# A hybrid encoder layer on one core: normalised tokens split in token rows and turned by transposing DMA transfers

## The chip, the core and the metric

The kernel runs on one core of one Trainium2 chip. A core has a matrix engine (TensorE, "PE" in the profile, with its weight loads as "PEld"), three elementwise engines (VectorE "DVE", ScalarE "ACT", GpSimd "POOL"), a queue engine (SyncE, "SP") that issues most transfers, and 16 DMA engines that carry them out. TensorE reads its operands from the on-chip memory SBUF and writes to PSUM. The metric is the device time of one execution in microseconds; lower is better.

## The reference

One layer over 2048 tokens of width 1024. Everything reads the same normalised tokens `h` through one input projection, and that is all that the change touches.

```python
def rms_norm(x, w):
    y = x32 * lax.rsqrt(jnp.mean(x32 * x32, axis=-1, keepdims=True) + EPS)
    return (y * w)

h = rms_norm(x, norm_pre_w)                       # (2048, 1024)
proj = h @ w_in                                   # (2048, 5648)
aq, ak, av, bqkv, ba, bb, mq, z = jnp.split(proj, pts, axis=-1)
# A: grouped-query attention on aq, ak, av; B: gated DeltaNet on bqkv, ba, bb
# M: cross-attention of mq into the memory tokens, whose keys and values are
mkv = rms_norm(mem, mem_norm_w) @ w_mem_kv        # (256, 1024)
x = x + rms_norm((concat([y_a, y_b, y_m]) * silu(z)) @ w_out, norm_post_w)
```

## The kernel before

Products of float32 precision are made from float16 parts: a number is split into a rounded part "hi" and a remainder "lo", and a product is the sum of three float16 products (hi·hi, hi·lo, lo·hi). The normalised tokens are needed with the 1024 channels on the partitions; that tensor, `hT`, is four tiles of 512 tokens (`hT0` to `hT3`), each with a hi and a lo part for eight blocks of 128 channels. `hT` is the operand of every projection: `tok_proj` takes 128 tokens of it as the stationary operand, `chan_proj` and `b_proj` take 512 tokens of it as the moving one.

The first stage (pool `s0`, about the first 118 us) does three things side by side.

- The memory tokens: `mem_load(g)` fetches a quarter of `w_mem_kv` in two halves (`mraw`, two buffers), ACT rounds each (`whi`), DVE or POOL makes the remainder (`wlo`), and `mem_group(g)` multiplies (tiles `mem`, 48 products in each of four groups).
- The tokens, in 16 blocks of 128. `tok_norm` loads two blocks (`x`, four buffers), ACT sums their squares (`jk_x`), DVE takes the inverse root in some eleven small operations (`rs_x`, `rs_u`, `rst`) and scales (`h`, three buffers). `tok_turn` turns a block with eight TensorE transposes into PSUM (`tp`); from there ACT writes the hi part and DVE the lo part into `hT`.
- The values: `av_proj` multiplies a turned block with 272 columns of weights (`av`, 24 products), ACT takes it out of PSUM (`ab`, `vt`), DVE takes a maximum (`vmax`), and SP stores `vt` to `v`.

A loop over blocks writes them in this order, with the turning two blocks and the values four blocks behind the loading:

```python
if i < TB and i % 2 == 0:
    tok_norm(i)
if 0 <= i - 2 < TB:
    tok_turn(i - 2)
if 0 <= i - 4 < TB:
    av_proj(i - 4)
```

The order on each engine is not this one: a scheduler that works on a model of the times reorders the instructions of every engine when the kernel is built, and each engine then runs its own list strictly in order, waiting for semaphores. SP is such a list too: a transfer that waits holds back all that stand behind it.

Two short chains cross the engines in this stage: the scale of the memory keys (`p2mk`) and that of the memory values (`p2mv`) each need a DVE maximum, a TensorE transpose, a DVE maximum, a TensorE product and four small DVE operations.

After this stage come the query and key projections with rotation (`q`, `qt`), the convolution and DeltaNet branch (`b` and others), the gates (`z`), and attention. Attention already uses transposing transfers: `low` sends the split probabilities `hl` (128 x 4096 float16, 32 blocks of 128 x 128; `hla` in the profile) through one `dma_start_transpose` on SP into `PT`.

Of the kernel before, what the change touches and what calls it, by code (L numbers as in the profile page):

```python
# [14 lines left out]
F16 = mybir.dt.float16  # L15
I32 = mybir.dt.int32
AF = mybir.ActivationFunctionType
ALU = mybir.AluOpType
# [5 lines left out]
D = 1024  # L24
# [4 lines left out]
KC = D // 128  # L29
# [8 lines left out]
def hybrid_layer(ctx: ExitStack, tc: tile.TileContext, t: dict, out, dbg=None):  # L38
    nc = tc.nc
# [17 lines left out]
    V, G, A, T, Q = (Engine(e) for e in (nc.vector, nc.gpsimd, nc.scalar, nc.tensor, nc.sync))  # L57
# [132 lines left out]
    hpool = ctx.enter_context(tc.tile_pool(name="hT", bufs=1))  # L190
# [12 lines left out]
    hT = []  # L203
# [35 lines left out]
    def chan_proj(ps, wg, u, tb4):  # L239
        n = 0  # L240
        for kc in range(KC):
            hi, lo = (w[:, kc % 4, u * 128:u * 128 + 128] for w in wg[kc // 4])
            for wt, ht in ((hi, 0), (hi, 1), (lo, 0)):
                T.matmul(ps, wt, hT[tb4][ht][:, kc, :], start=(n == 0), stop=(n == 3 * KC - 1))
                n += 1
                if n < 3 * KC:
                    yield
# [11 lines left out]
        return load_w(src, sum(n for _, n in segs), fac, fetch)  # L259

    def tok_proj(ps, wg, tb):
        hh, hl = hT[tb // 4]
        sl = slice((tb % 4) * 128, (tb % 4) * 128 + 128)
        n = 0
        for kc in range(KC):
            hi, lo = wg[kc // 4]
            for ht, wt in ((hh, hi), (hh, lo), (hl, hi)):
                T.matmul(ps, ht[:, kc, sl], wt[:, kc % 4, :], start=(n == 0), stop=(n == 3 * KC - 1))
                n += 1


    with tc.tile_pool(name="s0", bufs=1) as p:
# [5 lines left out]
        def turned(h, dst_hi, dst_lo, name):  # L278
            for half in range(2):
                ps = tp_ps(f"tp_{name}_{half}", (128, 4, 128))  # L280
                for k in range(4):
                    T.transpose(ps[:, k, :], h[:, (half * 4 + k) * 128:(half * 4 + k + 1) * 128], ident)
                split_evac(ps, dst_hi[:, half * 4:half * 4 + 4], dst_lo[:, half * 4:half * 4 + 4])
# [36 lines left out]
        for j in range(2):  # L320
            sl = slice(j * 128, j * 128 + 128)
# [31 lines left out]
        for g in range(4):  # L353
# [2 lines left out]
                wav, (avcs,) = load_group([(1280, 256), (3072, 16)], dma)  # L356
            mem_group(g, wg)
            wg = nxt
        hT.extend(hpool.tile([128, 2, KC, 512], F16, tag="B16", name=f"hT{b}", bufs=6, align_bytes=512).rearrange("p i k c -> i p k c") for b in range(4))
        hs = {}  # L360

        def tok_norm(tb):
# [10 lines left out]
                hs[tb + j] = scaled(xs[j], wpre, rst[:, j:j + 1], f"{tb + j}")  # L373

        def tok_turn(tb):
            sl = slice((tb % 4) * 128, (tb % 4) * 128 + 128)
            turned(hs.pop(tb), hT[tb // 4][0][:, :, sl], hT[tb // 4][1][:, :, sl], f"{tb}")

        def av_proj(tb):
            ps = mm_ps(f"av{tb}")  # L380
# [130 lines left out]
    with tc.tile_pool(name="s2", bufs=1) as p:  # L511
        wg, bcs, xbs, svs, kts_ = {0: nxt[0]}, {0: nxt[1]}, {}, {}, {}

        def b_proj(ch, b):
            g, u = ch // 2, ch % 2
            if u == 1 and b == 0:
                if g < 5:
                    wg[g + 1], bcs[g + 1] = load_group([(1536 + 256 * (g + 1), 256)])
                else:
                    wg[6] = z_load(4)  # L520
            if b == 0:
                xb = xbs[ch] = p.tile([128, S + 4], F32, tag="xb", name=f"xb{ch}", bufs=2)
                V.memset(xb[:, 0:2], 0.0)
                V.memset(xb[:, S + 2:S + 4], 0.0)
            ps = mm_ps(f"b{ch}_{b}")
            n = 0
            for kc in range(KC):
                hi, lo = wg[g][kc // 4]
                sl = slice(u * 128, u * 128 + 128)
                for wt, ht in ((hi, 0), (hi, 1), (lo, 0)):  # L530
                    T.matmul(ps, wt[:, kc % 4, sl], hT[b][ht][:, kc, :], start=(n == 0), stop=(n == 3 * KC - 1))
                    n += 1
            A.activation(xbs[ch][:, 2 + 512 * b:2 + 512 * (b + 1)], ps, AF.Copy, scale=bcs[g][0])

# [262 lines left out]
    with tc.tile_pool(name="s3a", bufs=1) as sv0:  # L797
        p = rows
# [685 lines left out]
```

## Time and profile before

| | |
|---|---|
| median of 3 runs | 2539.05 us (2533.95 to 2544.41) |
| the profiled execution: time / span of its trace | 2539.24 us / 2537.5 us |
| TensorE busy, share of the span | 2368.3 us, 93% |
| VectorE busy | 1827.2 us, 72% |
| ScalarE busy | 1270.5 us, 50% |
| GpSimd busy | 626.1 us, 25% |
| first `av` product / first `q` product after the stage | 52.32 us / 117.84 us |

A busy share is an average over stages with different limits. All times below are microseconds from the start of the span; a row "start, length" gives when a piece of work began and how long it ran, and a "[1.65 <-ACT whi]" behind it means that the engine had been idle for 1.65 us before and what ended that. Rows that merge several instructions show their count as "x12". Ends of TensorE rows overlap the next one, so a rate is best read from one start to the next.

### The profile page before, as it was taken

How to read it: one execution, taken by the hardware profiler on the slowest of the kernel's cores; microseconds unless marked ns; L12 is line 12 of the kernel's file. 1: busy time of each engine (PE TensorE's matmuls, PEld its weight loads, DVE VectorE, ACT ScalarE, POOL GpSimd, SP SyncE). 2: the span in 40 equal slices, each digit the busy share in tenths (PEclk: the TensorE clock that was granted, in tenths of full speed). 3: DMA queues.
4: the chain of work that ended last, by engine and by line, in shares of the span. 5: the costliest groups of instructions: out<-in, count | busy, mean ns of one | idle time of the engine just before them, and what ended most of it. 6: DMA issues, size and time to landing. Idle time of an engine off the chain costs nothing.

```text
span 2537.5 us, 42839 instructions
## 1 busy us (share of the span) xinstructions
PE 2368.3 (93%) x15989; PEld 1619.0 (64%) x15997; DVE 1827.2 (72%) x3434; ACT 1270.5 (50%) x2496; POOL 626.1 (25%) x450
## 2 busy tenths in 40 slices
PE   6989999999999898998999898899989899999998
PEld 6778974555444356666654566566656566778887
DVE  7778768999658835545545899999999899453332
ACT  5533335544443134554645776777778778211110
POOL 2154431112111220111121333333345333111110
PEclk9999999999999999999999999999999999999999
DMA  6431213234488456767766999999999999864441
GB/s 226 144 92 63 84 59 86 83 111 125 135 257 221 135 153 203 217 200 242 239 200 183 214 222 226 203 225 215 219 227 227 227 221 209 249 223 153 150 161 42
DMA packets 867375, 448.50 MB, mean 177 GB/s; under 512 B 639072, under 2 KB 816736, under 8 KB 866912
## 3 DMA queue, kind: packets, MB, share of 16 engines
q1 hardware_dynamic: 854720, 402.78, 61.4%
q0 software_dynamic: 12448, 43.00, 5.0%
q8 instruction: 126, 2.06, 0.3%
q14 instruction: 81, 0.66, 0.1%
HBM read 195.01 MB, written 108.07 MB: 119 GB/s over the span
## 4 chain that ended last, share of the span: by engine, by line
PE 27%; DVE 15%; issue 5%; DMA 4%; ACT 2%; SPq 1%; POOL 1%; ACTq 0%; DVEq 0%; POOLq 0%
PE o L51 12%; DVE mxa L51 7%; PE sa L51 6%; DVE hla L51 4%; PE pva L51 3%; PE z L51 3%; DVE misc L51 1%; DMA PT<-hla 1%; ACT Pa L51 1%; DMA Od<-oo 1%; DMA n<-NI 1%; DMA xx<-bx 1%; DVE mxm L51 1%; DMA wor<-in_w_out 1%; SPq L51 1%
## 5 line engine op out<-in xcount | busy, mean ns | idle before, releaser
L51 PEld LDWEIGHTS <-wparts 128*128 128x128 f16 x3072 | 293.9, 98 | 326.4 <-issue 15.8
L51 PE MATMUL sa<-K,qa 128*128 128x512 f16 x1536 | 375.2, 380 | 39.1 <-ACT Pa L51 36.4
L51 ACT ACTIVATE Pa<-sa,mxa,undo 128x1024 f32<-128x1024 f32 x256 | 305.9, 1199 | 189.2 <-DVE mxa L51 146.9
L51 PE MATMUL pva<-PT,V 128*128 128x256 f16 x3072 | 382.0, 275 | 13.0 <-DMA PT<-hla 12.1
L51 PE MATMUL z<-hT,wparts 128*128 128x512 f16 x1536 | 372.4, 383 | 0.3
L51 PEld LDWEIGHTS <-V 128*128 128x128 f16 x3072 | 301.3, 99 | 104.8 <-issue 21.9
L51 DVE TENSOR_REDUCE mxa<-sa 128x1 f32<-128x1024 f32 x256 | 305.4, 1212 | 42.8 <-PE sa L51 42.5
L51 PE MATMUL o<-wo,mhl 128*128 128x512 f32 x1416 | 328.4, 393 | 6.9 <-DVE mhl L51 2.6
L51 POOL TENSOR_TENSOR hla<-Pa,hla 128x768 f16<-128x768 f32 x128 | 215.2, 1681 | 452.8 <-ACT hla L51 367.9
L51 PEld LDWEIGHTS o<-wo,mhl 128*128 128x128 f32 x1416 | 266.1, 189 | 68.5 <-DVE mhl L51 3.9
L51 DVE TENSOR_TENSOR hla<-Pa,hla 128x1280 f16<-128x1280 f32 x128 | 279.4, 2183 | 6.8 <-ACT hla L51 5.1
L51 PEld LDWEIGHTS <-qa 128*128 128x128 f16 x1536 | 150.3, 98 | 178.1 <-issue 49.2
L51 PE MATMUL b<-hT,wparts 128*128 128x512 f16 x1152 | 256.8, 379 | 0.0
L51 ACT CAST hla<-Pa 128x2048 f16<-128x2048 f32 x128 | 242.3, 1893 | 9.4 <-DMA PT<-hla 9.4
L51 PEld LDWEIGHTS <-hT 128*128 128x128 f16 x2304 | 226.0, 98 | 31.6 <-DVE hT L51 1.2
L51 PE MATMUL q<-wparts,hT 128*128 128x256 f16 x1920 | 215.8, 275 | 0.0
L51 POOL TENSOR_SCALAR wraw<-wraw,wsc 128x1024 f32<-128x1024 f32 (+1 forms) x22 | 67.5, 3066 | 348.5 <-DVE wy L51 271.0
L51 DVE SCALAR_TENSOR_TENSOR y<-xb,convw,y 128x512 f32<-128x512 f32 x192 | 145.4, 772 | 1.7
L51 ACT CAST mhl<-mr 128x2048 fp32r<-128x2048 f32 (+1 forms) x16 | 29.2, 1826 | 228.6 <-PE o L51 210.3
L51 DVE TENSOR_TENSOR mhl<-mr,mhl 128x2048 fp32r<-128x2048 f32 (+1 forms) x16 | 35.1, 2191 | 134.8 <-ACT mhl L51 134.8
L77 POOL DMA_DIRECT2D gate<-zg x64 | 35.5, 554 | 374.6 <-DVE zg L51 205.5
L51 POOL TENSOR_TENSOR mg<-mg 128x1024 f32<-128x1024 f32 (+1 forms) x16 | 35.1, 2196 | 259.0 <-DMA mg<-r 222.9
(328 smaller groups left out, 3330.6 us busy)
## 6 DMA issues: line engine op xcount, KB each, us to landing
xx<-bx SPq DMA_DIRECT2D x64, 512.0 KB, 5.1
wraw<-in_w_in POOLq DMA_DIRECT2D x42, 512.0 KB, 5.5
gate<-zg POOLq DMA_DIRECT2D x64, 256.0 KB, 4.0
NI<-nit SPq DMA_DIRECT2D x32, 512.0 KB, 4.0
mr<-mix SPq DMA_DIRECT2D x13, 1024.0 KB, 5.6
x<-in_x SPq DMA_DIRECT2D x16, 512.0 KB, 4.9
qT<-qo SPq DMA_DIRECT2D x32, 256.0 KB, 2.5
qa<-qT SPq DMA_DIRECT2D x32, 256.0 KB, 3.5
```

The costliest lines, as they stand in the source:

```text
L51: ins = f(*args, **kw)
L77: nc.gpsimd.dma_start(to, of)
```

## The change

`tok_turn` no longer uses TensorE. A block `h` is split while it still has tokens on the partitions: ACT writes the hi part and DVE the lo part of a float16 tile `h16` (128 x 2 x 1024, two buffers), both from SBUF to SBUF. One transposing transfer on SP then turns its 16 blocks of 128 x 128 into `hT`. To receive it, `hT` is laid out as [partition, block of tokens, part, channel block, 128 tokens], so that one block of tokens is contiguous; a product that reads 512 tokens now reads four pieces of 128 that lie 4 KB apart. Nothing is left out of the computation.

```diff
-                T.matmul(ps, wt, hT[tb4][ht][:, kc, :], start=(n == 0), stop=(n == 3 * KC - 1))
+                T.matmul(ps.rearrange("p (b c) -> p b c", c=128), wt, hT[tb4][:, :, ht, kc, :], start=(n == 0), stop=(n == 3 * KC - 1))
...
-        hh, hl = hT[tb // 4]
-        sl = slice((tb % 4) * 128, (tb % 4) * 128 + 128)
+        hh, hl = (hT[tb // 4][:, tb % 4, i] for i in range(2))
...
-                T.matmul(ps, ht[:, kc, sl], wt[:, kc % 4, :], start=(n == 0), stop=(n == 3 * KC - 1))
+                T.matmul(ps, ht[:, kc, :], wt[:, kc % 4, :], start=(n == 0), stop=(n == 3 * KC - 1))
...
-        hT.extend(hpool.tile([128, 2, KC, 512], F16, tag="B16", name=f"hT{b}", bufs=6, align_bytes=512).rearrange("p i k c -> i p k c") for b in range(4))
+        hT.extend(hpool.tile([128, 4, 2, KC, 128], F16, tag="B16", name=f"hT{b}", bufs=6, align_bytes=512) for b in range(4))
...
         def tok_turn(tb):
-            sl = slice((tb % 4) * 128, (tb % 4) * 128 + 128)
-            turned(hs.pop(tb), hT[tb // 4][0][:, :, sl], hT[tb // 4][1][:, :, sl], f"{tb}")
+
+            h = hs.pop(tb)
+            h16 = p.tile([128, 2, D], F16, tag="h16", name=f"h16_{tb}", bufs=2, align_bytes=512)
+            A.copy(h16[:, 0], h)
+            V.tensor_tensor(h16[:, 1], h, h16[:, 0], op=ALU.subtract)
+            nc.sync.dma_start_transpose(hT[tb // 4][:, tb % 4].rearrange("p i k c -> p (i k) c"), h16.rearrange("p i c -> p (i c)"))
```

`b_proj` changes as `chan_proj` does. Beyond the first stage every engine's list is the same row for row; within it the scheduler has moved rows. In the names below, `x10`, `h16_6`, `vt4`, `av6` are those of token block 10, 6, 4 and 6.

The SP list, from the store of the fourth block of values to the last turned block. Before:

```order
L51 DMA v_65<-vt3_823 128x256
L51 DMA x11_948<-in_x 128x1024
L51 DMA x12_1087<-in_x 128x1024
L51 DMA v_65<-vt4_894 128x256
L51 DMA x13_1091<-in_x 128x1024
L51 DMA v_65<-vt5_938 128x256
L51 DMA v_65<-vt6_1009 128x256
L51 DMA x14_1202<-in_x 128x1024
L51 DMA x15_1206<-in_x 128x1024
L51 DMA v_65<-vt7_1053 128x256
```

Now, at the same place, the stretch that carries blocks 6 and 7 and the loads of 12 and 13:

```order
L51 DMA mv16_69<-mv16_668 128x2048
L380 DMA_TRANSPOSE hT1_480<-h16_6_794 128x16x128
L380 DMA_TRANSPOSE hT1_480<-h16_7_828 128x16x128
L51 DMA v_65<-vt5_858 128x256
L51 DMA x12_987<-in_x 128x1024
L51 DMA x13_991<-in_x 128x1024
L380 DMA_TRANSPOSE hT2_481<-h16_8_889 128x16x128
L51 DMA v_65<-vt6_919 128x256
L380 DMA_TRANSPOSE hT2_481<-h16_9_923 128x16x128
L51 DMA v_65<-vt7_953 128x256
```

and, directly behind it, the stretch with the last two loads:

```order
L380 DMA_TRANSPOSE hT2_481<-h16_10_1012 128x16x128
L51 DMA v_65<-vt8_1042 128x256
L51 DMA x14_1082<-in_x 128x1024
L380 DMA_TRANSPOSE hT2_481<-h16_11_1046 128x16x128
L51 DMA v_65<-vt9_1076 128x256
L51 DMA x15_1086<-in_x 128x1024
L380 DMA_TRANSPOSE hT3_482<-h16_12_1107 128x16x128
L51 DMA v_65<-vt10_1137 128x256
L380 DMA_TRANSPOSE hT3_482<-h16_13_1141 128x16x128
L51 DMA v_65<-vt11_1171 128x256
L51 DMA v_65<-vt12_1205 128x256
L380 DMA_TRANSPOSE hT3_482<-h16_14_1175 128x16x128
```

The loads of the last two blocks stood behind the store of the seventh block of values (`vt6`); now they stand behind the stores of the ninth and tenth (`vt8`, `vt9`) and behind the turning of block 11.

The DVE list from the scale of the memory values to the blocks behind it, now:

```order
L51 COPY p2mmv_656<-p2mv_659 128x1
L51 TENSOR_SCALAR p2emv_657<-p2mmv_656 128x1
L51 TENSOR_SCALAR scales_99<-p2emv_657 128x1
L51 TENSOR_SCALAR undo_100<-p2emv_657 128x1
L51 SCALAR_TENSOR_TENSOR h_6_695<-x6_674,rst6_673,wpre_117 128x1024
L51 SCALAR_TENSOR_TENSOR h_7_697<-x7_678,rst6_673,wpre_117 128x1024
L51 SCALAR_TENSOR_TENSOR mv16_668<-mvt_207,scales_99,mv16_668 128x1024
L51 TENSOR_REDUCE vmax_96<-vt4_824 128x1
L51 TENSOR_TENSOR h16_6_794<-h_6_695,h16_6_794 128x1024
```

Block 6 is scaled right behind that chain, as it was before; but the chain's product on TensorE (`p2mv` from `ones`), which stood in the third block of values, now stands in the fifth, behind eight of `av4`'s 24 products.

## Rows read from the trace of the kernel before

**Rows 1.** The page's first part: busy time, share of the span and instructions of an engine.

```profile
PE 2368.3 (93%) x15989; PEld 1619.0 (64%) x15997; DVE 1827.2 (72%) x3434; ACT 1270.5 (50%) x2496; POOL 626.1 (25%) x450
```

**Rows 2.** Busy time of each engine in four stretches of the first stage; the columns are PE, PEld, DVE, ACT, POOL (with instructions), then TensorE's granted clock (1 is 2.4 GHz, 0.5 is 1.2), the busy share of the DMA engines and GB/s.

```profile
38.00:47.00 9.00, 7.32 (x34) 7.06 (x35) 8.69 (x23) 6.06 (x10) 4.27 (x2) 0.50 0.49 166
47.00:58.00 11.00, 11.00 (x91) 10.60 (x91) 6.50 (x13) 2.32 (x4) 4.10 (x3) 0.98 0.53 179
58.00:88.00 30.00, 30.00 (x261) 25.91 (x259) 22.98 (x58) 20.43 (x46) 0.00 (x0) 1.00 0.44 144
88.00:118.00 30.00, 25.70 (x218) 21.29 (x218) 22.91 (x55) 17.13 (x38) 7.99 (x6) 1.00 0.43 139
```

**Rows 3.** TensorE in order of time through the stage: start, length, work.

```profile
35.63 0.50 PE L51 MATMUL mem<-whi,mT 128*128 128x256 f32 x2 [1.65 <-ACT whi L51]
37.89 0.58 PE L51 MATMUL mem<-wlo,mT 128*128 128x256 f32 x1 [1.75 <-DVE wlo L51]
38.27 0.63 PE L51 MATMUL mem<-whi,mT 128*128 128x256 f32 x2
...
38.91 0.63 PE L51 MATMUL mem<-whi,mT 128*128 128x256 f32 x2
...
42.66 2.77 PE L51 MATMUL tp<-ident,h 128*128 128x128 f32 x12
45.08 0.56 PE L51 MATMUL mem<-wlo,mT 128*128 128x256 f32 x1
...
53.26 0.40 PE L51 MATMUL mem<-whi,mT 128*128 128x256 f32 x2
...
53.61 0.40 PE L51 MATMUL mem<-whi,mT 128*128 128x256 f32 x2
...
57.21 2.14 PE L51 MATMUL av<-wparts,hT 128*128 128x272 f16 x17
59.19 0.60 PE L51 MATMUL tp<-ident,h 128*128 128x128 f32 x4
59.63 2.94 PE L51 MATMUL av<-wparts,hT 128*128 128x272 f16 x24
...
77.78 0.60 PE L51 MATMUL tp<-ident,h 128*128 128x128 f32 x4
...
109.62 8.39 PE L51 MATMUL av<-wparts,hT 128*128 128x272 f16 x71
117.84 3.77 PE L51 MATMUL q<-wparts,hT 128*128 128x256 f16 x33
```

**Rows 4.** Groups of instructions between 20 and 120 us: count, busy time, mean ns of one, idle time before them.

```profile
L51 PE MATMUL av<-wparts,hT 128*128 128x272 f16 x384 | 48.3, 279 | 1.5 <-DVE hT L51 0.9 <-ACT hT L51 0.6
...
L51 DVE TENSOR_TENSOR hT<-tp,hT 128x512 f16<-128x512 f32 x32 | 20.9, 681 | 0.5 <-ACT hT L51 0.5
L51 DVE SCALAR_TENSOR_TENSOR h<-x,rst,wpre 128x1024 f32<-128x1024 f32 x16 | 20.1, 1280 | 0.6 <-DMA mkT<-mk 0.5
L51 PE MATMUL tp<-ident,h 128*128 128x128 f32 x128 | 18.7, 288 | 2.5 <-DVE wy L51 1.1 <-DVE h L51 0.8 <-DVE hT L51 0.6
L51 ACT CAST hT<-tp 128x512 f16<-128x512 f32 x32 | 17.4, 588 | 1.2 <-PE tp L51 1.2
...
L51 ACT ACTIVATE jk_x<-x 128x1024 bf16<-128x1024 f32 x13 | 13.7, 1057 | 14.0 <-DMA x<-in_x 14.0
...
L51 DVE TENSOR_REDUCE vmax<-vt 128x1 f32<-128x256 f32 x16 | 6.6, 413 | 8.1 <-ACT vt L51 8.0
...
L51 DVE TENSOR_TENSOR wlo<-mraw,whi 128x1024 fp32r<-128x1024 f32 x3 | 3.7, 1217 | 0.0
```

**Rows 5.** The transposing transfers of attention (`PT`): SP's time for one (min/median/max ns), the time to landing; the DVE remainders beside POOL in attention; and the token loads of 512 KB each between 20 and 120 us, their median time to landing.

```profile
L1158 SPq DMA_TRANSPOSE PT<-hla x128: 3844/4294/8226, 1376.0 to 2169.0; - x128
...
DMA to landing us min/median/max: 5.5/6.4/11.1
...
L51 DVE TENSOR_TENSOR hla<-Pa,hla x128: 1477/2230/2866, 1373.6 to 2164.0; 128x1280 f16<-128x1280 f32 x128
...
x<-in_x SPq DMA_DIRECT2D x12, 512.0 KB, 3.8
```

**Rows 6.** TensorE on moving operands of two pieces (`pva`, from `PT`) and of one piece (`q`), each up to the start of the next row.

```profile
1622.86 1.47 PE L51 MATMUL pva<-PT,V 128*128 128x256 f16 x12
1624.17 1.46 PE L51 MATMUL sa<-K,qa 128*128 128x512 f16 x6
...
299.75 8.68 PE L51 MATMUL q<-wparts,hT 128*128 128x256 f16 x78
308.26 1.04 PE L51 MATMUL qt<-ident,qr 128*128 128x128 f32 x8
```

**Rows 7.** Other engines in order of time: the last remainder of the memory weights on POOL; an ACT cast of 128 x 1024 from SBUF; small DVE operations of the inverse root; SP's issue of the last two token loads.

```profile
47.08 2.43 POOL L51 TENSOR_TENSOR wlo<-mraw,whi 128x1024 fp32r<-128x1024 f32 x1 [4.81 <-ACT whi L51]
...
101.75 1.06 ACT L51 CAST wparts<-wraw 128x1024 f16<-128x1024 f32 x1
...
83.69 0.16 DVE L51 TENSOR_TENSOR rs_u<-rs_u,rs_x 128x2 f32<-128x2 f32 x1
83.89 0.16 DVE L51 SCALAR_TENSOR_TENSOR rst<-rs_u,rst 128x2 f32<-128x2 f32 x1
...
86.72 1.53 SPq L51 DMA_DIRECT2D x<-in_x  x2
```

More of the change, by code (lines that the diff above doesn't have):

```diff
@@ L530, in b_proj @@
                 for wt, ht in ((hi, 0), (hi, 1), (lo, 0)):
-                    T.matmul(ps, wt[:, kc % 4, sl], hT[b][ht][:, kc, :], start=(n == 0), stop=(n == 3 * KC - 1))
+                    T.matmul(ps.rearrange("p (b c) -> p b c", c=128), wt[:, kc % 4, sl], hT[b][:, :, ht, kc, :], start=(n == 0), stop=(n == 3 * KC - 1))
                     n += 1
```

## The prediction

> **What bounds the kernel now.** I read the busy shares first: TensorE is busy for 93% of the span [rows 1], so time that it gets back counts unless something else takes its place. The change touches the first 118 us alone, so I then read the stretches of that stage [rows 2]. From 58 to 88 us TensorE has work for all 30.00 us while VectorE is at 22.98 and the DMA engines are below half. From 88 to 118 it has 25.70 of 30. In this stretch TensorE ends last, and nearly the only engine that waits for transfers is ScalarE, 14.0 us for token loads [rows 4]. Before 47 us it is the other way round: TensorE waits for ACT and DVE to split the memory weights (1.65 and 1.75 us) and runs at half clock [rows 2, 3].
>
> The stage ends for TensorE at 117.84, when the first `q` product starts [rows 3]. Everything behind stands in the same order as before, and its loads wait for the end of this stage, so I take it that a shift of this end moves the whole rest by the same amount. The question is where that end will lie.
>
> **What the change removes.** TensorE loses 128 transposes. Four of them take 0.44 us from 59.19 to 59.63, 0.11 each; twelve at half clock take 2.42 us from 42.66 to 45.08 [rows 3]. That is 116 × 0.11 + 2.42 = 15.2 us. On ACT two casts of 0.59 from PSUM go and one of 1.06 from SBUF comes; on DVE two remainders of 0.68 go and one of 128 x 1024 comes, for which the nearest row is `wlo` with 1.22 [rows 4, 7]. If POOL is active beside it, the row for attention bounds it: 2.23 for 1280 columns, 1.8 for 1024 [rows 5]. I take 1.22, since POOL has nothing to do from 58 to 88 us [rows 2]. ACT and DVE thus keep their load.
>
> **What it adds.** Sixteen transposing transfers on SP. None of this size is in the trace. The nearest are those of attention with twice the blocks: SP is held 4.29 us (median), the data has landed after 6.4 [rows 5]. By halves: SP 2.15, then a tail of 6.4 − 4.3 = 2.1, so 4.2 from issue to landing. Bounds: 3.2, if everything halves, and 6.4, if nothing does; those rows come from a stretch in which the DMA engines are much fuller, so I stay below the middle.
>
> Per block of 128 x 128 this is 4.2 / 16 = 0.26 us against TensorE's 0.11. The Trainium skill, page "VectorE: DVE Perf Modes", section "The three transpose paths", speaks against the change outright: it gives 1309 ns for a block through the DMA crossbar and 390 on TensorE, and its "Rules for kernel authors" tells to use TensorE wherever a PSUM destination will do. By its figure a transfer of 16 blocks would take an estimated 21 us; the attention rows, with 32 blocks in 6.4 us, speak against that.
>
> The moving operand in four pieces I cost at nothing: twelve `pva` products on two pieces take 1.31 us from start to start, 0.109 each, and 78 `q` products on one piece 8.51 us, also 0.109 [rows 6]. More pieces than two are not in the trace; the lower bound is nothing, the upper a rival below.
>
> **The new chain, step by step.** Without transposes TensorE is early, so the end is set by when `hT` arrives. I follow the new lists with durations from the rows.
>
> 1. Memory groups. POOL's last `wlo` ends at 49.5 [rows 7]; it hangs on loads that now partly queue behind transposing transfers, so I leave it there. TensorE reached the products that need it only at 53.05, held up by sixteen transposes and a half clock. Now it is there in time and needs 57.21 − 53.05 = 4.2 us: the groups end at 53.7 instead of 57.21.
> 2. A block of values costs 24 × 0.116 = 2.78 us (71 products from 109.62 to 117.84). Blocks 1 to 5 end at 53.7 + 5 × 2.78 = 67.6, ten us ahead of before (77.78) [rows 3]. Blocks 4 and 5 are turned in time by my count.
> 3. Block 6. Its scaling stands on DVE behind `p2mv`, whose product now stands behind eight products of `av4`: 53.7 + 3 × 2.78 + 0.9 = 63. Then four small operations (0.2 each, [rows 7]), `h_6`, `h_7`, the split of `mv16` (1.28 each, as `h`), `vmax` 0.41 and the remainder 1.22: 69.3. Plus 4.2: 73.5. TensorE idles for 5.9 us. Idle pieces of 1.65 and 1.75 were followed by a stretch at 0.50 of the clock [rows 2, 3]; there a group of three memory products took 0.64 us (38.27 to 38.91), against 0.35 later. So I let `av6` take 1.8 × 2.78 = 5.0: it ends at 78.5.
> 4. Block 9. `x12` is issued behind the transfers of blocks 6 and 7 (69.3 + 4.3 + `vt5`: 74) and lands 3.8 later by the row [rows 5], 4.4 with what is queued ahead. ACT sums its squares (1.25) ahead of `vt6`, and the store of `vt6` stands on SP ahead of the transfer of block 9: 78.4 + 1.25 + 0.75 + 0.35 = 80.8, landed at 85.0, `av9` ends at 87.8. (Block 8 is in by 80.5.)
> 5. Blocks 10 and 11. The squares of `x13` follow `vt6` on ACT and are done at 82.0; seven small operations and the remainder of block 10 (1.4 + 1.22) end at 84.6, the block lands at 88.8, `av10` ends at 91.6. Before the remainder of block 11 DVE's list holds a `vmax`, four small operations, two scalings, one more small one and another `vmax`: 0.41 + 0.8 + 2.56 + 0.2 + 0.41 + 1.22 = 5.6, so 90.2; landed at 94.4. Blocks 12 and 13 follow closely, landed at 97.5 and 100.5 behind `x15` on SP, and `av13` ends at 103.3.
> 6. Block 14. `x15` stands behind the transfer of block 11 (90.2 + 2.15) and the store of `vt9`: 92.9, against 88 before (two issues from 86.72 on, 1.53 long, [rows 7]). Load 4.4, squares 1.25, `vmax` and eleven small operations 2.6, two scalings 2.56, `vmax` 0.41, remainder 1.22, transfer 4.2: landed at 109.6. TensorE has idled for 6.3 us by then.
> 7. Two blocks are left: 5.6 us at full clock, 10 at half: 115.2 to 119.6. The middle, one block slow, is **117.4**, against 117.84.
>
> So the 15 us of transposes, and the 3.5 us won in the memory groups, are paid back as waits for blocks 6, 9 to 11 and 14. The sum is −0.4 us. On the profiled execution's 2539.24 us that is 2538.8; this execution lies 0.2 above the median of the runs, so I say **2539**.
>
> **Its own range.** Transfers at 3.2 and loads at 3.6 instead of 4.4, with full clock at the end, take off about 5 + 1.6 + 2.2 = 9 us (five transfers and two loads stand on the chain). Transfers at 6.4 that also hold SP for 4.3, remainders at 1.8 and both last blocks slow add 11 + 2 + 2 = 15, of which transfers at 5 would be half. 2530 to 2550.
>
> **Rivals.**
>
> *TensorE simply stays the bound* (faster). If the blocks arrive in time, TensorE runs through: 53.7 + 15 × 2.78 = 95.4, 22 us earlier, **2517**. For it: the stage is TensorE's in [rows 2], DVE had a quarter of its time free. Against it: the new SP list, where each transfer stands behind a store that needs an earlier block of values, and the place of `x15`. To gain 0.5% (12.7 us, about what a measurement of this kernel can tell from no change), block 14 would have to land by 99.5, ten us before my sum. Chance 0.09.
>
> *The transfers are dear* (slower). Five stand on the chain one behind the other (6, 9, 11, 14, 15). The whole is 0.5% slower when one costs (12.7 + 0.4) / 5 = 2.6 us more than 4.2, so from 6.8 on, which is just above the median of the large ones and below their longest, 11.1 [rows 5]. At 7.5 the end moves by 16.5 us: **2555**. For it: loads of tokens run between them on the same DMA engines. Against it: half the data, and those engines are at 0.44. Chance 0.16, a quarter of it still within 0.5%. By the Trainium skill's figure of the section cited above, sixteen transfers in a row on SP would take an estimated 334 us, the stage would end some 240 us later and the kernel near 2780; the rows of attention leave that one chance in a hundred, which is counted in this rival's.
>
> *The four pieces cost something* (slower). By the code 3072 products of 512 columns follow (`b`, `mq`, `z`); 4.3 ns each would decide, 10 ns would give 31 us, **2570**. Two pieces showed nothing. Chance 0.03.
>
> **How the numbers follow.** Forecast 0.72, and all of it within 0.5%; faster rival 0.09, of which 0.07 beyond 0.5%; dear transfers 0.16, of which 0.12 beyond; pieces 0.03. That makes faster 0.07, within 0.5% 0.78, slower 0.15. The range leaves out the ends of the rivals: 2530, the low end of my chain, to 2553, where most of the dear transfers are still in.
>
> **What would show it.** The groups `mem` end near 54 and `av5` near 68; TensorE waits some 6 us for block 6 and again for block 14, named as waits for a DMA into `hT`; the granted clock drops after these; `x15` is issued near 93; the first `q` product starts at 117 ± 9, and everything behind is shifted by one constant. `pva`-like rates for `b` and `z` (0.216 per product) stay. I am wrong if TensorE runs through with short waits (95 to 105), if a transfer takes over 6.8, or if `z` has another rate.

## The result

The changed kernel is slower by a little: 2544.44 us median against 2537.94 for the kernel before, taken beside it, ratio 1.0027 with an interval of 1.0015 to 1.0040, so 3.8 to 10.2 us. The time lies in the stated range and within 0.5%, but it moved by more than the runs are uncertain, and I had it standing still (2539).

The page of the changed kernel, first part, answers to [rows 1]. TensorE has lost its 128 transposes:

```profile
PE 2364.1 (93%) x15861; PEld 1609.1 (63%) x15869; DVE 1827.6 (72%) x3418; ACT 1272.0 (50%) x2480; POOL 629.1 (25%) x450
```

The stretches of [rows 2], with the same columns (PE, PEld, DVE, ACT, POOL, granted clock, DMA share, GB/s), for the changed kernel:

```profile
38.00:47.00 9.00, 6.80 (x44) 6.50 (x44) 8.87 (x12) 6.35 (x9) 5.95 (x2) 0.69 1.00 269
47.00:58.00 11.00, 9.97 (x84) 8.90 (x84) 10.61 (x26) 5.29 (x8) 4.02 (x3) 1.00 0.84 242
58.00:88.00 30.00, 21.05 (x166) 16.62 (x164) 21.98 (x56) 16.28 (x30) 0.00 (x0) 0.89 0.97 242
88.00:118.00 30.00, 20.52 (x140) 15.14 (x138) 19.34 (x40) 17.79 (x34) 9.14 (x6) 0.83 0.80 211
```

No compute engine is the bound from 58 to 118 us: TensorE has fallen from 30.00 and 25.70 to 21.05 and 20.52, VectorE is not fuller than before. What has risen is the DMA share, from 0.44 and 0.43 to 0.97 and 0.80.

TensorE in order of time, as in [rows 3]:

```profile
51.76 0.38 PE L51 MATMUL p2mk<-p2mmk,ones 1*128 1x1 f32 x2 [1.03 <-DVE p2mmk L51]
...
56.23 6.43 PE L51 MATMUL av<-wparts,hT 128*128 128x272 f16 x54
...
66.14 4.81 PE L51 MATMUL av<-wparts,hT 128*128 128x272 f16 x40
77.94 7.31 PE L51 MATMUL av<-wparts,hT 128*128 128x272 f16 x48 [6.99 <-DMA hT<-h]
87.21 7.40 PE L51 MATMUL av<-wparts,hT 128*128 128x272 f16 x48 [1.96 <-DMA hT<-h]
...
99.46 2.95 PE L51 MATMUL av<-wparts,hT 128*128 128x272 f16 x24 [2.05 <-DMA hT<-h]
106.94 8.15 PE L51 MATMUL av<-wparts,hT 128*128 128x272 f16 x48 [4.53 <-ACT wparts L51]
120.16 8.36 PE L51 MATMUL av<-wparts,hT 128*128 128x272 f16 x48 [5.07 <-DMA hT<-h]
128.36 3.77 PE L51 MATMUL q<-wparts,hT 128*128 128x256 f16 x33
```

The rows with waits begin with blocks 6, 8, 11, 12 and 14. (The wait at 106.94 is named after ACT's work on the next weights, which these products don't read; what they still lacked was the transfer of block 12, which landed at 106.90.) The stage ends at 128.36 instead of 117.84, 10.5 us later. The rest is shifted: the first `b` product stands at 373.09 instead of 363.20. The profiled execution, 2554.45 us, is among the longest three of twenty, and behind the stage single executions differ by several us where the kernels are alike (from the first `q` product to the first of attention 1243.5 us here, 1239.6 before, 1233.7 in the run with the stores off SP below). So the 10.5 us and the 6.5 us between the medians don't contradict each other.

The turned blocks (SP's time for one, then the time to landing) and the token loads, which answer to [rows 5]:

```profile
L380 SPq DMA_TRANSPOSE hT<-h x16: 1591/2366/4498, 28.9 to 118.0; - x16
...
DMA to landing us min/median/max: 4.0/5.4/6.9
...
x<-in_x SPq DMA_DIRECT2D x12, 512.0 KB, 4.0
```

The two landing figures rest on few transfers: the view has a landing for two of the sixteen turned blocks (block 8's 6.9 and block 15's 4.0) and for three of the twelve token loads, as in [rows 5]. The semaphore updates in the trace, sixteen for each transfer, give a landing for all of them: the turned blocks landed after 3.7 to 8.9 us, 4.7 in the middle, and the token loads after 4.7, against 4.1 before. Below, landings are told by these updates; where an expectation says 5.4, it is the view's figure.

### The profile page after: what moved, and what is told of

Read it like the earlier page. It is cut to its first block, busy times and chain, and to the rows that moved or that the text cites. A ratio compares the mean times of both kernels' runs of the same rounds, so it can differ in the third digit from the quotient of the medians.

```text
span 2552.7 us, 42601 instructions
## 1 busy us (share of the span) xinstructions
PE 2364.1 (93%) x15861; PEld 1609.1 (63%) x15869; DVE 1827.6 (72%) x3418; ACT 1272.0 (50%) x2480; POOL 629.1 (25%) x450
```

## The experiments

Theory A: the loss is a loop of waits (two buffers of `h16`, stores ahead of transfers on SP, the order on ACT and DVE), with TensorE's half clock behind each wait. Theory B: a transfer is dearer than I put it, because it fills the DMA engines. Theory C: the four pieces of the moving operand cost something. "First q" below is the start of the first `q` product in one profiled execution.

**Layout alone** (TensorE turns the tokens, into the new layout).

```diff
-            h = hs.pop(tb)
-            h16 = p.tile([128, 2, D], F16, tag="h16", name=f"h16_{tb}", bufs=2, align_bytes=512)
-            A.copy(h16[:, 0], h)
-            V.tensor_tensor(h16[:, 1], h, h16[:, 0], op=ALU.subtract)
-            nc.sync.dma_start_transpose(hT[tb // 4][:, tb % 4].rearrange("p i k c -> p (i k) c"), h16.rearrange("p i c -> p (i c)"))
+            turned(hs.pop(tb), hT[tb // 4][:, tb % 4, 0], hT[tb // 4][:, tb % 4, 1], f"{tb}")
```

> Only the layout of hT is changed; the turning stays on TensorE, and its casts and remainders write from PSUM straight into the new layout, so every product of 512 columns reads four pieces. Theory A (the loss is a loop of waits around the turned blocks) and theory B (the transfers themselves are dear): no change against the kernel before, 0 within 3 us; first q product at 118, 0.216 us per product of b and z. Theory C (the four pieces cost something): the whole loss of 6.8 us or more, spread over b, mq and z, at 2 ns or more for each of the 3072 products.

Measured 1.0006 (0.9990 to 1.0022), first q at 115.09. The groups of `b` and `mq` behind the stage in this kernel (count | busy, mean ns of one):

```profile
L51 PE MATMUL b<-hT,wparts 128*128 128x512 f16 x1152 | 256.8, 379 | 0.0
L51 PE MATMUL mq<-hT,wparts 128*128 128x512 f16 x384 | 86.3, 384 | 0.1
```

The same groups in the kernel before:

```profile
L51 PE MATMUL b<-hT,wparts 128*128 128x512 f16 x1152 | 256.8, 379 | 0.0
L51 PE MATMUL mq<-hT,wparts 128*128 128x512 f16 x384 | 86.0, 383 | 0.1
```

The third such group, `z`, is busy for 375.0 us here and 372.4 before, but for 370.3 in the half of the blocks below, which reads the same four pieces. So no cost of the four pieces shows: theory C is out, and the loss belongs to the turning. (The stage of this kernel ends 2.8 us earlier than before, without a gain in the time.)

**Stores off SP.**

```diff
-            dma(v_d[tb], vt)
+            wdma(v_d[tb], vt)
```

> The stores of the values go through the queue of GpSimd; SP carries loads and turned blocks alone. Theory A: the turned blocks 9, 11, 13 and 14 and the load of x15 no longer stand behind a store that waits for an earlier block of values; x15 is issued about 6 us earlier (91 instead of 97.5), block 14 lands 3 to 6 us earlier, and the first q product starts at 122 to 125 instead of 128.4. Theory B: the transfers still take 5.4 us each on DMA engines that stay nearly full (0.97), so the first q product stays within 1.5 us of 128.4 and the time at 1.003 of before.

Measured 1.0037 (1.0020 to 1.0053), first q at 128.53: not better. SP no longer waits for stores. The last five transfers stand in 23.48 us with nothing else between them; they hold SP for 14.6 of these, and over all sixteen the landing is 5.7 us in the middle instead of 4.7:

```profile
99.09 23.48 SPq L380 DMA_TRANSPOSE hT<-h  x5
```

Taking the stores out of SP's list thus won nothing. The test is not a clean one: GpSimd's list, which now carries the stores, also issued its weight loads elsewhere, two at 76.18 beside block 6, which landed after 7.8 us (6.0 in the changed kernel), and two at 111.28 beside block 14 (8.4 instead of 3.9).

**A third buffer of the split tile.**

```diff
-            h = p.tile([128, D], F32, tag="h", name=f"h_{name}", bufs=3)
+            h = p.tile([128, D], F32, tag="h", name=f"h_{name}", bufs=2)
-            h16 = p.tile([128, 2, D], F16, tag="h16", name=f"h16_{tb}", bufs=2, align_bytes=512)
+            h16 = p.tile([128, 2, D], F16, tag="h16", name=f"h16_{tb}", bufs=3, align_bytes=512)
```

> The split tile h16 has three buffers instead of two; to make room h (and the two memory tiles that share its place) has two instead of three. Theory A: the cast of a block no longer waits for the landing of the block two before it (5.5 us of waits on ACT, and 2.1 ahead of block 8), so blocks 8, 10 and 12 land some 2 us earlier each and the first q product comes 2 to 5 us earlier than 128.4. Theory B: landing times go by the DMA engines, which are full either way; within 1.5 us of 128.4.

Measured 1.0075 (1.0051 to 1.0099, from four executions), first q at 134.99: slower, which neither theory said. Up to block 11 the transfers go as in the changed kernel or a little earlier (block 11's is issued at 93.30 instead of 94.73), but block 12's is issued at 103.11, beside four weight loads of GpSimd's queue (issued from 101.91 to 104.94), and TensorE waits for it until 121.49. It landed after 18.3 us, block 13's after 14.3, and the last two of those loads after 16.3 and 17.0. TensorE's row, then two stretches, in whose last columns the DMA engines are counted full, yet move little (the share adds up the time of the packets, and passes 1 where an engine has several under way):

```profile
121.49 13.66 PE L51 MATMUL av<-wparts,hT 128*128 128x272 f16 x96 [21.08 <-DMA hT<-h]
...
108.00:112.00 4.00, 0.00 (x0) 0.00 (x0) 2.63 (x4) 2.10 (x3) 0.00 (x0) 0.50 1.30 115
112.00:116.00 4.00, 0.00 (x0) 0.00 (x0) 0.00 (x0) 0.00 (x0) 0.00 (x0) 0.50 1.15 130
```

The edit also took a buffer from `h`, so it does not test the loop cleanly; it points at transfers beside loads.

**Half of the blocks.** Odd blocks by transfers, even ones on TensorE.

```diff
+            if tb % 2 == 0:
+                return turned(h, hT[tb // 4][:, tb % 4, 0], hT[tb // 4][:, tb % 4, 1], f"{tb}")
```

> Even blocks are turned by TensorE as before, odd blocks by transfers. Theory A: with eight transfers none waits for a buffer that was filled just before, and block 14 no longer hangs on a transfer; TensorE saves 7 us of transposes and waits little: first q product at 110 to 116, the kernel 2 to 8 us faster than before. Theory B: the eight transfers still land after 5.4 us, but the DMA engines are at about 0.7 instead of 0.97, and landing falls to 4 to 4.5 us; first q product at 113 to 119, the kernel within 4 us of before.

Measured 0.9969 (0.9955 to 0.9982), 5 to 11 us faster than the kernel before, first q at 114.52. The eight transfers still land after 5.6 us in the middle (3.6 to 7.9), and the DMA share is 0.90 from 58 to 88, but TensorE waits only 2.4 us for transfers between 56 and 128 (16.1 in the changed kernel, and 4.5 more for block 12 under another name):

```profile
58.00:88.00 30.00, 27.11 (x231) 22.43 (x230) 25.47 (x66) 21.02 (x43) 0.00 (x0) 1.00 0.90 240
88.00:118.00 30.00, 25.80 (x200) 20.98 (x199) 20.70 (x43) 15.51 (x32) 8.74 (x7) 0.89 0.64 179
```

Where the gain comes from is not all shown: the profiled stage ends 3.3 us before that of the kernel before, and within 1 us of the layout kernel's 115.09, which gained nothing in time.

**The price of a transfer.** Useless transfers behind the query stage of the layout kernel.

```diff
+        for i in range(3):
+            nc.sync.dma_start_transpose(da, src)
...
+        for i in range(4):
+            nc.sync.dma_start_transpose(db[i], src)
...
+        dma(ld[0], t["x"][0, 0:128, :])
+        nc.sync.dma_start_transpose(dc[0], src)
...
+        for i in range(4):
+            dma(ld[1 + i], t["x"][0, 128 * i:128 * i + 128, :])
+        nc.sync.dma_start_transpose(dc[1], src)
```

> The price of a transfer by itself. Into the layout kernel (all turning of tokens on TensorE) nine transposing transfers of the same size (128 x 2048 float16, 16 blocks) from a constant tile are added behind the query stage, where the DMA engines are at 0.2 to 0.3: three one after the other, each waiting for the landing of the one before; four in a row without waits; one behind a load of 512 KB; one behind four loads of 512 KB. They feed nothing. Theory A (waits in a loop; a transfer itself costs what I put, 4.2 us): alone 4 to 4.4 us, four in a row about 2.2 us apart, behind one load 4.5, behind four loads under 6. Theory B (a transfer is dear): alone 5.4 or more, or four in a row 4 us or more apart, since each fills the DMA engines, and behind four loads 8 or more.

SP's issues in order of time:

```profile
383.11 5.65 SPq L506 DMA_TRANSPOSE pa<-psrc  x2
...
398.03 1.62 SPq L506 DMA_TRANSPOSE pa<-psrc  x1
401.92 7.87 SPq L509 DMA_TRANSPOSE pb<-psrc  x4
```

Alone, the third of the first group is read by VectorE at 401.73: 3.7 us. The four in a row start at 401.92 and the last at 408.0, so 2.03 us apart, and land 3.8 to 4.2 after their issue. So far my price stands (4.2 and 2.15). Behind one load of 512 KB it took 6.1 us (412.42 to 418.56), behind four 8.9 (420.59 to 429.45). The second of the first group, issued at 387.44, had landed only when the third was issued at 398.03: 10.6 us. No load was meant to be there, but GpSimd had issued two weight loads at 387.45. Alone theory A is right, beside loads theory B.

At 512 KB in 2.03 us a transfer moves 258 GB/s. The Trainium skill, page "DMA: Bandwidth & Descriptors", section "Latency and other measured facts", gives 261 GB/s for transposing transfers with a middle dimension that is not contiguous and some 350 to 400 for the contiguous case; the measured rate is near the first and below the second. The 1309 ns a block that the prediction cited from another of its pages does not agree with this run (2.03 / 16 = 0.127 us a block, alone 0.23).

**No idle TensorE.**

```diff
+            for i in range({6: 48, 12: 36, 14: 40}.get(tb, 0)):
+                T.matmul(ps[:, 0:272], hT[(tb - 2) // 4][:, (tb - 2) % 4, 0, i % KC, :], wav[0][0][:, 0, :], start=True, stop=True)
             tok_proj(ps[:, 0:272], wav, tb)
```

> What the half clock costs. The changed kernel, with products that nobody uses ahead of the values of blocks 6 (48 of 272 columns), 12 (36) and 14 (40), on operands that are there already, so that TensorE does not stand idle while it waits for these blocks. If the half clock behind the waits is part of the loss (theory A), the granted clock stays at 1.00 through these blocks, two blocks take 5.6 us instead of 7.7 to 8.4, and the first q product starts 3 to 6 us before 128.4: the kernel within 3 us of before. If TensorE's clock does not matter, since the next block is late anyway (theory B), the first q product stays at 128.4 within 1 us.

Measured 1.0040 (1.0026 to 1.0054), first q at 133.55. The filler did its work up to 88 us: granted clock 1.00 (0.89 in the changed kernel), blocks 6 and 7 in 5.73 us. But block 8 was not there, and TensorE waited for it until 89.17, later than 87.21:

```profile
66.80 10.37 PE L51 MATMUL av<-wparts,hT 128*128 128x272 f16 x88
78.96 5.73 PE L51 MATMUL av<-wparts,hT 128*128 128x272 f16 x48 [1.79 <-DMA hT<-h]
89.17 7.00 PE L51 MATMUL av<-wparts,hT 128*128 128x272 f16 x48 [4.48 <-DMA hT<-h]
```

So in the middle the half clock did not set the time, since the next block was late anyway. At the end the test failed: block 13's transfer, issued at 106.08 beside two GpSimd loads (106.74), landed at 118.7, 12.6 us later. What the half clock of the last two blocks costs (8.20 instead of 5.57 us) stays open.

**The first six blocks only.** Blocks 6 to 15 on TensorE (`if tb >= 6: return turned(...)`).

> Blocks 0 to 5 are turned by transfers, blocks 6 to 15 by TensorE as before. By theory A the loss sits in the late blocks, whose transfers stand in a loop with the stores and the casts; the early ones cost nothing, save TensorE 48 transposes (6.6 us with the half clock) and bring the memory groups forward: first q product at 109 to 114, the kernel 4 to 9 us faster than before. By theory B the early transfers also compete with the loads of the memory weights and of the tokens: the groups end later than 56, and the first q product is at 115 to 119, within 3 us of before.

Measured 0.9973 (0.9960 to 0.9986), first q at 116.01. The groups end at 56.54, as in the changed kernel, so they do not come forward by the transfers, and first q is where theory B had it; the time is better than theory B said.

**Weight loads later.** Two of GpSimd's loads go through SP, behind block 13.

```diff
-                        nxt = load_group([((which + g) * 256 if which + g < 4 else 1536, 256)])
+                        nxt = load_group([((which + g) * 256 if which + g < 4 else 1536, 256)], dma if which == 0 else None)
```

> Two of the four weight loads of 512 KB that GpSimd issues at 99.2 and 104.1 us, beside the transfer of block 12, go through SP instead, behind the transfer of block 13. If the contention of these loads makes block 12 late (theory B in part: a transfer is dear beside loads), block 12 lands within 5.5 us of its issue instead of 8.9, the values of block 12 start 3 us earlier, and with the casts of blocks 14 and 15 no longer behind the squares of that weight group on ScalarE the first q product comes 3 to 6 us earlier than 128.4. If block 12 is late by its place in the loop alone (theory A), the first q product moves by less than 1.5 us.

Measured 1.0021 (1.0006 to 1.0036), first q at 126.08. Block 12's transfer is issued at 100.76 and its values start at 107.06, at most 6.3 us later instead of 8.9; the first q product gains 2.3 us in the profile, between the two theories, and the time cannot be told from that of the changed kernel. These loads are a part of the loss, not the whole.

**The load without the waits.** The layout kernel with sixteen useless transfers, set off by a one-column copy of `h`.

```diff
+            idle = p.tile([128, 2 * KC, 128], F16, tag="idle", name=f"idle{tb}", bufs=2, align_bytes=512)
+            V.tensor_copy(idle[:, 0, 0:1], h[:, 0:1])
+            nc.sync.dma_start_transpose(idle.bitcast(mybir.dt.uint16), wpre.bitcast(mybir.dt.uint16))
```

> The load of sixteen transfers without the waits for them. The layout kernel (TensorE turns the tokens; first q product at 115.1) also issues, for every block, one transposing transfer of the same size from a constant tile into a tile that nobody reads, on SP, as soon as the block is scaled. Theory B in the form that the runs so far left (each transfer fills the 16 DMA engines for 2 us or more; with the token loads, the stores and the weight loads that is more than the stage has): the DMA engines go from 0.5 to 0.9 or more between 58 and 118 us, token loads land after 5 us or more instead of 3.8, and the first q product comes 4 to 10 us later than 115.1 although nothing waits for a transfer. Theory A (the loop of waits): the first q product stays within 2 us of 115.1, the kernel within 3 us of before.

Measured 1.0031 (1.0015 to 1.0047): a loss as large as the changed kernel's, though no product waits for a transfer (VectorE waits 2.5 us in all for the place to copy into). First q is at 123.26, but here `q` products stand among the last `av`; by the first `b` product, 372.14 against 359.57 in the layout kernel, the stage is 12.6 us longer. ACT waits 25.4 us for token loads (14.5 in the layout kernel), and TensorE 9.6 us for remainders of the memory weights (7.4 there). It is not the changed kernel's loss in all parts: 5.3 us of the 12.6 are there when the memory groups end (60.99 against 55.72), which in the changed kernel end 1 us earlier than before. Nor is it the DMA engines' work alone: the token loads land after 4.5 us (4.1 in the layout kernel), but SP, which the transfers hold, issues the last two at 103.63 instead of 84.17. Two stretches:

```profile
58.00:88.00 30.00, 27.48 (x223) 23.48 (x222) 17.49 (x46) 15.13 (x33) 0.00 (x0) 0.94 0.86 204
88.00:118.00 30.00, 25.10 (x201) 21.00 (x200) 23.35 (x67) 19.47 (x41) 7.97 (x6) 0.94 1.04 249
```

**The waits with half of the load.**

```diff
+        for b in range(4):
+            G.memset(hT[b][:, :, 1], 0.0)
...
-            nc.sync.dma_start_transpose(hT[tb // 4][:, tb % 4].rearrange("p i k c -> p (i k) c"), h16.rearrange("p i c -> p (i c)"))
+            nc.sync.dma_start_transpose(hT[tb // 4][:, tb % 4, 0], h16[:, 1])
```

> The waits without half of the load. The changed kernel, but a transfer turns the remainders alone (8 blocks of 128 x 128, into the place of the hi part; the place of the lo part is zero), so the output is not that of the reference; casts, remainders, buffers, stores and the order of the waits stay. Theory B: the DMA engines fall from 0.97 to 0.75 or less between 58 and 88, transfers land within 3.5 us instead of 5.4, and the first q product comes at 108 to 118 instead of 128.4. Theory A: each of some five transfers on the chain gets 1 to 1.5 us shorter and the loop stays: 121 to 125.

Measured 0.9993 (0.9979 to 1.0007), first q at 113.91 instead of 128.36. The order of the waits is still there, and the hi parts are not turned at all. A transfer holds SP for 1.25 us in the middle:

```profile
L382 SPq DMA_TRANSPOSE hT<-h x16: 1231/1253/3328, 29.2 to 107.2; - x16
...
58.00:88.00 30.00, 20.24 (x159) 15.94 (x156) 28.19 (x60) 22.28 (x40) 8.25 (x4) 0.90 0.99 289
88.00:118.00 30.00, 28.55 (x230) 23.34 (x231) 19.30 (x46) 13.29 (x27) 0.74 (x1) 0.93 0.50 131
```

The DMA share did not fall to 0.75 before 88 us, as I had expected: the work came earlier, and the second stretch is at 0.50. In the first, blocks 4 to 9 landed after 2.9 to 6.0 us (3.7 to 6.9 in the changed kernel); the six behind them took 2.7 to 3.4. Of GpSimd's weight loads two went out at 77.03 and none beside blocks 12 and 13. So more than the size of a transfer differs: most of the late blocks found no load beside them.

**One transfer beside loads, by itself.** In the layout kernel, behind the query stage; before each round VectorE reads all that has landed and writes a column of `src` and of both `ld`, which sets off the next.

```diff
+        for fetch in (None, wdma, wdma, dma, dma, None, wdma, dma):
...
+            if fetch is not None:
+                for i in range(2):
+                    fetch(ld[i], t["w_in"][0, 512 * i:512 * i + 512, 1024:1280].rearrange("(k p) c -> p k c", p=128))
+            nc.sync.dma_start_transpose(dst, src)
```

> The price of one transfer beside weight loads, by itself: in the layout kernel, behind the query stage, transfers of 16 blocks from a constant tile, each set off by VectorE when all that went before has landed: four alone one after the other; then one alone, two together with two weight loads of 512 KB each on GpSimd's queue, two behind two such loads on SP's own queue, one alone, one with GpSimd's loads, one behind SP's. If it is the DMA engines' work alone that adds up, 2 us for a transfer and 1.6 for a load, all of these with loads end 3 to 4 us later than one alone (3.8), at 7 to 8 us, on either queue. If transfers and the loads of GpSimd's queue hinder each other, as the 10.6 us of one transfer between 387 and 398 us of the run before would have it, those with GpSimd's loads take 10 us or more and those behind SP's loads 6 to 8.

VectorE's reads of the landed block, alone (first row), beside GpSimd's loads (two rows) and behind loads on SP (two rows); SP issued these transfers at 408.51, 412.90, 420.93, 429.39 and 437.95:

```profile
412.21 0.16 DVE L51 COPY psrc<-pdst 128x1 f16<-128x1 f16 x1 [3.73 <-DMA pdst<-psrc]
...
418.92 0.16 DVE L51 COPY psrc<-pdst 128x1 f16<-128x1 f16 x1 [6.04 <-DMA pdst<-psrc]
...
427.76 0.16 DVE L51 COPY psrc<-pdst 128x1 f16<-128x1 f16 x1 [6.86 <-DMA pdst<-psrc]
...
436.36 0.16 DVE L51 COPY psrc<-pdst 128x1 f16<-128x1 f16 x1 [7.56 <-DMA pdst<-psrc]
...
444.76 0.16 DVE L51 COPY psrc<-pdst 128x1 f16<-128x1 f16 x1 [7.75 <-DMA pdst<-psrc]
```

3.7 us alone, then 6.0, 6.8, 7.0 and 6.8; later repeats took 7.6 beside GpSimd's loads and 6.9 behind SP's. So two loads add 2.3 to 3.9 us, alike on either queue, and the 10 us that the earlier run suggested beside GpSimd's loads do not come back in these rounds. (Ahead of them, one of the first four transfers, issued at 394.83 beside two weight loads that GpSimd had issued at 393.99, landed after 9.1.) It is the work of the DMA engines that adds up. That agrees with the Trainium skill, same page, section "Issuing engines are not separate DMA queues": queues of different engines end on the same 16 DMA engines.

**A mixture.** Blocks 0 to 5, 7, 9 and 11 by transfers (`if tb % 2 == 0 and tb >= 6 or tb >= 12: return turned(...)`).

> A candidate: blocks 0 to 5, 7, 9 and 11 by transfers, blocks 6, 8, 10 and 12 to 15 by TensorE: nine transfers, none of them in the last stretch with the weight loads of GpSimd's queue. Theory B: the DMA engines keep room (0.8 or less from 58 to 118), the first q product at 110 to 115, the kernel 5 to 10 us faster than before. Theory A: blocks 7, 9 and 11 still wait in turn, first q product at 114 to 119, 2 to 7 us faster.

Measured 0.9974 (0.9959 to 0.9989), not to be told from the half. First q is at 107.77, here too ahead of the last values; the first `b` product is at 357.79, 5.4 us earlier than before. Three divisions of the work beat both kernels, the half by 8 us against the kernel before.

## Why the prediction failed

The steps, forecast and measured in the changed kernel (us; "values" is TensorE's start on that block):

| step | forecast | measured |
|---|---|---|
| 1, memory groups end | 53.7 | 56.23 |
| 3, block 6 issued, values | 69.3, 73.5 | 71.92, 77.94 |
| 4, block 8 values; block 9 issued | by 80.5; 80.8 | 87.21; 84.98 |
| 5, block 11 issued, values | 90.2, 94.4 | 94.73, 99.46 |
| 5, block 12 values | 97.5 | 106.94 |
| 6, `x15` issued; block 14 issued, values | 92.9; 105.4, 109.6 | 97.47; 116.25, 120.16 |
| 7, first `q` product | 117.4 | 128.36 |

The course is the forecast one: TensorE is early, waits some 7 us for block 6 and 5 for block 14, runs at half clock behind these, and the transposes' 15 us are paid back as waits. The step that failed is one term, **T = 4.2 us from issue to landing**, taken as the same for every transfer. From issue to values block 6 took 6.0 us, block 8 6.9, block 11 4.7, block 12 8.9, block 14 3.9: together 9.5 us more than five times 4.2. That is not the 11.0 us by which the end is late, piece for piece, since the five don't all stand on one chain. By the table the lateness is 2.5 us after step 1, 4.4 at the values of block 6, 5.1 at those of block 11, 9.4 at those of block 12 and 10.9 at the issue of block 14; the largest piece is block 12's transfer. SP's issues of these blocks and of the token loads ahead of them, then GpSimd's weight loads:

```profile
71.92 6.02 SPq L380 DMA_TRANSPOSE hT<-h  x2
78.66 1.24 SPq L51 DMA_DIRECT2D x<-in_x  x2
80.30 3.97 SPq L380 DMA_TRANSPOSE hT<-h  x1
84.98 2.15 SPq L380 DMA_TRANSPOSE hT<-h  x1
...
94.73 1.83 SPq L380 DMA_TRANSPOSE hT<-h  x1
...
97.47 0.42 SPq L51 DMA_DIRECT2D x<-in_x  x1
98.00 4.50 SPq L380 DMA_TRANSPOSE hT<-h  x1
...
116.25 3.59 SPq L380 DMA_TRANSPOSE hT<-h  x2
...
99.24 1.55 POOL L77 DMA_DIRECT2D wraw<-in_w_in  x2
...
104.08 1.52 POOL L77 DMA_DIRECT2D wraw<-in_w_in  x2 [0.30 <-POOL wparts L51]
```

Over all sixteen transfers T was not far off (4.7 in the middle). It left out what is under way when a transfer is issued: the seven blocks issued with no load or store of 512 KB under way (3, 5, 7, 9, 10, 14, 15) landed after 3.7 to 4.1 us, the nine others after 4.7 to 8.9. Block 12's transfer was issued 0.5 us behind the load of `x15`. In the DMA packets of the trace this load runs from 99.22 to 102.27, the transfer from 101.04 to 104.08, and the first two of GpSimd's loads from 103.81 to 106.66; the transfer landed at 106.90.

The error was not in the price of one transfer: alone it is 3.7 and in a row 2.03, even below what I took. It was that I costed it as a delay alone and let it run for nothing on the DMA engines, with the sentence that they "are at 0.44". From 58 to 118 us, in the columns of [rows 2], the kernel before:

```profile
58.00:118.00 60.00, 55.70 (x478) 47.20 (x477) 45.90 (x112) 37.56 (x82) 7.99 (x6) 1.00 0.44 141
```

The changed kernel:

```profile
58.00:118.00 60.00, 41.57 (x304) 31.76 (x301) 41.32 (x96) 34.07 (x63) 9.14 (x6) 0.86 0.89 227
```

Before, the DMA engines work 26.4 of 60 us. Ten transfers (in the changed kernel those of blocks 4 to 13 are issued there, and block 14's at its very end), at my own 2.15 on SP, make that 47.9, or 0.80; measured are 53.4. With the engines that busy, more than half of the transfers met loads or stores of their neighbours. The numbers for it were all on the table. My bounds for T (3.2 to 6.4) and the rival of dear transfers had the mechanism, but with 6.8 as the point where it decides by 0.5%, and they left the middle at 4.2. That the time still came out inside the range is partly luck: the range allowed for dearer transfers, but on a path by `x15`, while block 14 hung on block 12 (below).

That the load of sixteen transfers can make a loss of this size without a product that waits for one is shown by the idle transfers (1.0031), though in part by another way. The half data (0.9993) show that the loop's order of waits need not make a loss; there the late blocks also met fewer loads, so it doesn't show that the size of the transfers alone decides. What the runs don't separate is the DMA engines' time from SP's: in the changed kernel a transfer held SP for 1.6 to 2.2 us with no load or store of 512 KB under way, and for 1.8 to 4.5 with one.

Other misses. Step 1 (2.5 of the 11.0 us): TensorE stood until 51.76 for `p2mk`, whose VectorE operations stand behind one of two columns that took 2.22 us instead of 0.16, while GpSimd made its remainder (47.51 to 49.86); I had counted no such delay. The row of the changed kernel:

```profile
47.67 2.22 DVE L51 TENSOR_SCALAR rst<-rs_x 128x2 int32<-128x2 int32 x1
```

Step 4: I overlooked that the cast of a block waits for the landing of the block two before it, since `h16` has two buffers. Step 6: block 14 did not hang on `x15` but on block 12. ACT's list has the values of block 12 ahead of the casts of blocks 14 and 15, and these values ran at half clock behind the late landing. DVE had scaled blocks 14 and 15 by 108.76, and their casts began at 113.92. ACT in order of time in the changed kernel, the cast of block 8, then block 12's values and the casts of 14 and 15:

```profile
77.97 1.04 ACT L51 CAST h<-h 128x1024 f16<-128x1024 f32 x1 [2.08 <-DMA hT<-h]
...
112.35 0.27 ACT L51 ACTIVATE ab<-av,wc 128x16 f32<-128x16 f32 x1 [5.42 <-PE av L51]
...
113.92 1.98 ACT L51 CAST h<-h 128x1024 f16<-128x1024 f32 x2
```

Right were: TensorE not the bound any more, the four pieces free, the rest shifted (first `b` by 9.9 us), the loss of the transposes' gain to waits for blocks 6 and 14, and the half clock behind them.

## What to carry to other kernels

A transfer has two prices: its delay, and its time on the DMA engines that all queues share. Before work is moved there, add the second to the share that the stretch already has (here 0.44 became 0.89 from 58 to 118 us, while the three divisions that gained time stayed at 0.55 to 0.77). And cost a landing by what is under way at its issue: here 3.7 to 4.1 us with no load of 512 KB under way, 4.7 to 8.9 with one. Then move only so much: half of the turning on each side beat both all and none.

## What the runs showed of the hardware that I had not expected

A transposing transfer of 512 KB landed after 3.7 us alone and after 6.0 to 7.6 beside two loads of 512 KB, but in four cases beside GpSimd's loads after 9.1, 10.5, 12.6 and 18.3. In the last, the DMA engines were counted busy throughout while they moved 115 and 130 GB/s (108 to 116 us), where transfers in a row move 258. In the trace's packets these four are spread out, with GpSimd's packets among them: the packets of one transfer take 5.1 to 12.0 us from first to last, where they take 2.0 alone. Block 12's in the changed kernel (8.9 us) took 3.0, nearly all ahead of GpSimd's. Mixing alone does not tell them apart, since some transfers that landed after 6.8 to 7.6 us had such packets among theirs as well; why some cases are so much worse was not settled.

Half the data (8 blocks) landed after 2.7 us with no load under way, against 3.7 for the whole, but after up to 6.0 with loads under way.
